# A two-block sequence model on one core: Hyena's convolution by a folded transform at odd frequencies, and the second layer's modulation in the third feed-forward layer

## The chip, the core and the metric

The kernel runs on one core of one Trainium2 chip. A core has a matrix engine (PE, with its weight loads written PEld), a vector engine (DVE), a scalar engine (ACT), a general engine (POOL), and a queue engine (SP) that issues most transfers. The metric is the device time of one execution in microseconds. Three runs of the kernel before took 2188.26, 2190.82 and 2191.55 us; their median is 2190.82.

## The reference

The first block is two layers of feed-forward, a convolution and recurrence mixer, and feed-forward again, on 256 tokens of width 1024. The second block has two layers that are modulated by a condition: an even one (attention and Hyena) and an odd one (mLSTM). The change touches the modulation and Hyena's convolution:

```python
def adaln(cond, w_mod, b_mod):
    m = jax.nn.silu(cond) @ w_mod + b_mod
    return _split(m, (D_MODEL, D_MODEL, D_MODEL))

def bidir_long_conv(u, filt):            # n = 256, filt has 2n taps
    uf = jnp.fft.rfft(u.astype(jnp.float32), n=2 * n, axis=1)
    ff = jnp.fft.rfft(filt, axis=0)
    return jnp.fft.irfft(uf * ff[None], n=2 * n, axis=1)[:, :n].astype(u.dtype)

g = v * x1                               # in hyena_mixer
out = x0 * (bidir_long_conv(g, filt) + g * hy_bias)
```

It is done for 256 latent and 256 context tokens, 1024 channels each, with one filter per channel. The modulation is a product of one vector (the condition, for latents and for the context) with a 1024 x 3072 matrix in each of the two layers.

## The kernel before

Every number is fp32, and a product of two matrices is done as three matrix instructions on halves (`mm3`, lines 127, 128, 129): high by high, high by low, low by high. `split` makes the halves: ACT casts to the high one (L96), DVE subtracts it (L97). `wload` brings 1 MB of weights by one transfer (tile `raw`, two buffers) and splits it into `wh` and `wl` (six buffers each). PSUM banks are in three rings: `mm` (2), `tp` (2, transposes), `acc` (4). A scheduler sets the order of the instructions of each engine from the program and from its own estimates; `weave` and `chain` in the program only say which pieces may lie beside which.

In the trace the stages are: first feed-forward layer 0 to 213 us (beside it the filter's spectrum, `hyena_filter`, four groups of 256 channels, matrix products at 154 to 206); mixer to 464; second feed-forward layer to 655 (beside it the first layer's modulation: 48 reductions in L537, all of them here, although the program gives the second half of them to the third layer); third feed-forward layer to 845; mixer to 1093; fourth feed-forward layer to 1287 (beside it the context's normalization, `ctx_start`); attention to 1495; Hyena to 1835; mLSTM to the end.

`modulation` (line 518) brings the condition (`cb`), forms its silu (ACT L526, DVE L527 and L528) and then takes, for each 128 rows of the transposed matrix (`mraw`, 512 KB each), a multiply-and-sum over 1024 columns in DVE (L537). Its result `mod` scales and shifts the normalized tokens, and gives the gain of the layer's output (`gain_out`, `gain_rows`, through DRAM).

Hyena takes four groups of 256 channels. `project(g)` has eight pieces of 24 matrix instructions (`mm<-HT,w`, 512 columns), each followed by a short convolution on ACT and DVE (`dwconv`) or a gate, and ends in `gg`, the convolution's input, with channels on partitions and 2 x 256 tokens on the free axis. Beside the projection of group g runs the convolution of group g-1: `turn` transposes `gg` (8 transposes, L1001) into `gT`; `forward` multiplies it by cosine and sine tables (`dft`), two halves of frequencies (`kt`) of 12 matrix instructions of 512 columns each, multiplies by the filter's spectrum `F` in DVE (L1019, L1020, L1021) and splits the result into `Y`; `back` multiplies with `Y` as the stationary and the table as the moving operand, 48 matrix instructions of 256 columns, so that channels come back to partitions; ACT scales (`z`, L1040), DVE adds the bias term and the gate (L1041, L1042) and splits `hyo`; `rows` multiplies `hyo` by the output's weights. The second layer's modulation (40 reductions) is woven into groups 0 to 3 too.

The last group has no projection beside it. It goes in two halves of 256 columns, latents and then context; each ends in `next_layer` (line 659), a chain of squares, a power on POOL, a scaling and transposes (L181) that write `HT`, the mLSTM's input. mLSTM's gate products (`acc<-w,HT`) are there to fill PE.

The lines of the profile are those of this kernel:

## Time and profile before

| | us |
|---|---|
| median of three runs | 2190.82 |
| profiled execution, its own time | 2189.3 |
| its span, first to last instruction | 2187.5 |
| PE busy | 2123.8 (97%) |
| PEld busy | 1866.8 (85%) |
| DVE busy | 1595.0 (73%) |
| ACT busy | 1076.1 (49%) |
| POOL busy | 148.0 (7%) |

A matrix instruction's duration in the trace runs over into the next one, which starts before it has ended. What one costs PE is therefore the distance between two starts, which is shorter than the mean duration of a group of rows. [...]

### The profile page before, as it was taken

Reading aid. Unit: us, or ns where it says so; the run is one execution under the profiler, and the core shown is the slowest. Engines: PE = TensorE matmul, PEld = TensorE weight load, DVE = VectorE, ACT = ScalarE, POOL = GpSimd, SP = SyncE. Lnnn points to the kernel's source line nnn. Section 1 sums busy time; section 2 is a strip of 40 time slices with the busy share of each in tenths; the row PEclk is TensorE's granted clock in tenths of the full one; section 3 lists DMA queues with packets and bytes.
Section 4 is the critical chain, followed back from the end, with each engine's and each line's share of the span. In section 5 each row is a group of like instructions: output and inputs, shape, how many; then the busy total and the mean of one; then the engine's idle time right before and its main releaser. Section 6 shows DMA issues by size and latency. Waiting matters only on the chain.

```text
span 2187.5 us, 32454 instructions
## 1 busy us (share of the span) xinstructions
PE 2123.8 (97%) x12945; PEld 1866.8 (85%) x12945; DVE 1595.0 (73%) x2600; ACT 1076.1 (49%) x1650; POOL 148.0 (7%) x137
## 2 busy tenths in 40 slices
PE   8999999999999999999999999999999989999997
PEld 8988897889989997998889976888888867788886
DVE  7665777689977656777576668765898687876766
ACT  5554556544435544575455444544333345565653
POOL 0000221000000000220010012000000022000001
PEclk9999999999999999999999999999999999999999
DMA  8554554567765555546555543114444224233441
GB/s 290 197 185 148 207 188 154 198 240 258 274 248 193 193 186 184 199 154 212 203 187 180 193 161 116 58 40 154 169 159 173 87 75 159 96 116 114 147 141 70
DMA packets 65503, 366.67 MB, mean 168 GB/s; under 512 B 7935, under 2 KB 13128, under 8 KB 27848
## 3 DMA queue, kind: packets, MB, share of 16 engines
q1 hardware_dynamic: 65352, 364.61, 47.5%
q8 instruction: 101, 1.65, 0.3%
q14 instruction: 50, 0.41, 0.1%
HBM read 361.40 MB, written 3.18 MB: 167 GB/s over the span
## 4 chain that ended last, share of the span: by engine, by line
PE 79%; DVE 10%; ACT 4%; POOL 3%; issue 2%; DMA 2%; SPq 0%; POOLq 0%; DVEq 0%; ACTq 0%
PE mm L127 13%; PE mm L128 13%; PE mm L129 13%; PE acc L129 12%; PE acc L128 12%; PE acc L127 12%; DVE wl L97 4%; ACT wh L96 2%; DMA raw<-in_w 1%; PE tp L181 1%; POOL HT L97 1%; DVE v L255 1%; DVE bst L256 1%; PE tp L127 1%; POOL rsv L119 0%
## 5 line engine op out<-in xcount | busy, mean ns | idle before, releaser
L97 DVE TENSOR_TENSOR wl<-raw,wh 128x1024 fp32r<-128x1024 f32 (+1 forms) x566 | 706.3, 1259 | 269.1 <-ACT wh L96 266.4
L96 ACT CAST wh<-raw 128x1024 fp32r<-128x1024 f32 (+1 forms) x590 | 605.7, 1046 | 463.4 <-PE acc L129 153.6
L127 PE MATMUL mm<-xT,wh 128*128 128x256 f32 x1048 | 294.3, 281 | 5.9 <-ACT wh L96 5.9
L129 PE MATMUL mm<-xT,wl 128*128 128x256 f32 x1048 | 294.1, 281 | 3.0 <-POOL wl L97 2.7
L128 PE MATMUL mm<-xT,wh 128*128 128x256 f32 x1048 | 293.6, 280 | 0.0
L129 PE MATMUL acc<-xT,wl 128*128 128x256 f32 x856 | 239.8, 280 | 2.3 <-DVE u L423 1.1
L127 PE MATMUL acc<-xT,wh 128*128 128x256 f32 x856 | 239.9, 280 | 0.7 <-ACT wh L96 0.7
L128 PE MATMUL acc<-xT,wh 128*128 128x256 f32 x856 | 239.5, 280 | 0.0
L127 PEld LDWEIGHTS mm<-xT,wh 128*128 128x128 f32 x1048 | 197.8, 189 | 6.9 <-ACT wh L96 6.3
L129 PEld LDWEIGHTS mm<-xT,wl 128*128 128x128 f32 x1048 | 197.7, 189 | 3.8 <-POOL wl L97 3.1
L128 PEld LDWEIGHTS mm<-xT,wh 128*128 128x128 f32 x1048 | 197.7, 189 | 0.2
L127 PE MATMUL mm<-HT,wh 128*128 128x512 f32 (+1 forms) x448 | 171.2, 382 | 0.9 <-DVE vv L97 0.9
L129 PE MATMUL mm<-HT,wl 128*128 128x512 f32 (+1 forms) x448 | 170.3, 380 | 0.0
L128 PE MATMUL mm<-HT,wh 128*128 128x512 f32 (+1 forms) x448 | 170.2, 380 | 0.0
L129 PEld LDWEIGHTS acc<-xT,wl 128*128 128x128 f32 x856 | 160.9, 188 | 3.1 <-DVE u L423 1.5
L127 PEld LDWEIGHTS acc<-xT,wh 128*128 128x128 f32 x856 | 160.9, 188 | 0.9 <-ACT wh L96 0.9
L128 PEld LDWEIGHTS acc<-xT,wh 128*128 128x128 f32 x856 | 160.9, 188 | 0.0
L127 PE MATMUL acc<-wh,ht 128*128 128x512 f32 x352 | 139.5, 396 | 0.0
L129 PE MATMUL acc<-wh,ht 128*128 128x512 f32 x352 | 139.5, 396 | 0.0
L128 PE MATMUL acc<-wl,ht 128*128 128x512 f32 x352 | 139.3, 396 | 0.0
L127 PE MATMUL mm<-wh,HT 128*128 128x512 f32 x288 | 114.7, 398 | 0.0
L128 PE MATMUL mm<-wl,HT 128*128 128x512 f32 x288 | 114.0, 396 | 0.0
(488 smaller groups left out, 4401.5 us busy)
## 6 DMA issues: line engine op xcount, KB each, us to landing
raw<-in_w SPq DMA_DIRECT2D x131, 1024.0 KB, 4.8
raw<-in_wi_cvb SPq DMA_DIRECT2D x24, 1024.0 KB, 4.8
mraw<-in_w_mod SPq DMA_DIRECT2D x48, 512.0 KB, 4.4
raw<-in_wi_g SPq DMA_DIRECT2D x16, 1024.0 KB, 4.8
raw<-in_e_hy SPq DMA_DIRECT2D x16, 1024.0 KB, 5.1
raw<-in_o_oz SPq DMA_DIRECT2D x16, 1024.0 KB, 4.8
raw<-in_e_out SPq DMA_DIRECT2D x10, 1024.0 KB, 4.8
raw<-in_wi_r SPq DMA_DIRECT2D x8, 1024.0 KB, 4.8
```

Of the source, the lines that this page charges most:

```text
L96: S.copy(h, src)
L97: eng.tensor_tensor(l, src, h.bitcast(F32), op=ALU.subtract)
L127: TE.matmul(p, lhsT=lh, rhs=rh, start=first, stop=False)
L128: TE.matmul(p, lhsT=lh, rhs=rl, start=False, stop=False)
L129: TE.matmul(p, lhsT=ll, rhs=rh, start=False, stop=last)
L181: TE.transpose(tp[:, i * P : (i + 1) * P], b, ident)
L255: V.scalar_tensor_tensor(v[:, c], acc[h], coef, xa[t][:, c], op0=ALU.mult, op1=ALU.add)
L256: V.bn_stats(st[:, h, :], v[:, c])
```

## The change

The transform has odd frequencies, at which the wrap-around of a cyclic convolution comes with the opposite sign, and time is taken apart into even and odd samples. One table of 128 x 128 for each of cosine and sine and for each of even and odd samples then serves both halves of the frequencies: the one half is the sum and the other the difference of the even and the odd part. So

- `forward` has 12 matrix instructions of 512 columns instead of 24 (four `acc` banks); then two copies on ACT, four sums or differences of 512 columns on DVE, the products with `F` (four of 1024 columns, four sums of 512), and two sums or differences of 1024 columns that fold the spectrum, before the four splits of `Y`;
- `back` has the table as the stationary operand: 12 matrix instructions of 512 columns instead of 48 of 256, two copies on ACT into `zt`, and 8 transposes (L1077) that bring channels back to partitions; ACT's `z` reads these and writes every second column;
- `turn` reads every second column of `gg` as its stationary operand, and the filter reads every second column of `hd`;
- the filter's spectrum takes 12 matrix instructions of 256 columns in a group instead of 24, two scalings on ACT, two sums or differences of 512 columns on DVE, and one transfer instead of two;
- the second layer's modulation is the third feed-forward layer's side work, and all of the first layer's is the second's; the second layer's `gain_out` goes from the mLSTM's second head to the fourth feed-forward layer;
- a few tiles (`gb`, `hyo`, `xc`) have other places.

```diff
+    def turned(pool):
+        gain_out(pool.tile([P, P], F32, tag="gr", name="gr"), 1, 0)
+        yield
...
     def dft_tables(pool, n, raw):
 
-        d = [pool.tile([P, 2, n, 256], F32R, tag=f"dft{i}", name=f"dft{i}") for i in range(2)]
-        for k in range(2):
-            for i in range(n // 2):
-                r = raw([P, 2, 256])
-                nc.sync.dma_start(r, a["dft"][:, k, 2 * i : 2 * i + 2])
-                split(d[0][:, k, 2 * i : 2 * i + 2], d[1][:, k, 2 * i : 2 * i + 2], r)
+        d = [pool.tile([P, n, P], F32R, tag=f"dft{i}", name=f"dft{i}") for i in range(2)]
+        for i in range(0, n, 4):
+            m = min(4, n - i)
+            r = raw([P, 2, 256]).rearrange("p a n -> p (a n)")[:, : m * P].rearrange("p (a n) -> p a n", a=m)
+            nc.sync.dma_start(r, a["dft"][:, i : i + m])
+            split(d[0][:, i : i + m], d[1][:, i : i + m], r)
         return d
...
-                        p[:, s * 256 : (s + 1) * 256], hd[:, 0, tsl(pt)], hd[:, 1, tsl(pt)], w3s[:, 0, s, :], w3s[:, 1, s, :],
+                        p[:, s * 256 : (s + 1) * 256], hd[:, 0, pt::2], hd[:, 1, pt::2], w3s[:, 0, s, :], w3s[:, 1, s, :],
...
-            for kt in range(2):
+
+            eo = []
+            for pt in (1, 0):
                 p = psum("tp").rearrange("p (s n) -> p s n", s=2)
                 for s in range(2):
-                    btile(
-                        p[:, s, :],
-                        [(dft[0][:, pt, s, tsl(kt)], dft[1][:, pt, s, tsl(kt)]) for pt in range(2)],
-                        lambda pt: (pq[pt][:, 0, s, :], pq[pt][:, 1, s, :]),
-                    )
-                F = t2([P, 2, 256], "F")
-                S.copy(F, p)
-                nc.sync.dma_start(fdram[g][:, kt], F)
+                    c = 2 * pt + s
+                    mm3(p[:, s, :], dft[0][:, c], dft[1][:, c], pq[pt][:, 0, s, :], pq[pt][:, 1, s, :], True, True)
+                x = t2([P, 2, 256], f"eo{pt}")
+                S.mul(x, p, 1.0 / 256)
+                eo.append(x)
+            F = t2([P, 2, 2, 256], "F")
+            for hf, op in enumerate((ALU.add, ALU.subtract)):
+                V.tensor_tensor(F[:, hf], eo[1], eo[0], op=op)
+            nc.sync.dma_start(fdram[g], F)
...
+        def pair(s, nm):
+            return s.pool.tile([P, 2, 512], F32, tag="pr", name=nm, bufs=4)
+
         def turn(s, g, segs, gT):
 
             for t in range(2):
                 tp = psum("tp")
                 for i, st in enumerate(segs):
                     for j in range(2):
-                        TE.transpose(tp[:, i * 256 + j * P :][:, :P], s.gg[g][j][:, st * T + t * P :][:, :P], ident)
+                        TE.transpose(
+                            tp[:, i * 256 + j * P :][:, :P], s.gg[g][j][:, st * T + t : (st + 1) * T : 2], ident
+                        )
                 split(gT[t][:, 0, :], gT[t][:, 1, :], tp[:, : 256 * len(segs)])
 
         def forward(s, n, gT, Y, bank="acc"):
 
-            seg = lambda x: x.rearrange("p (s n) -> p s n", s=n)
-            for kt in range(2):
-                u = []
+
+            w = 256 * n
+            ps = {}
+            for t in (1, 0):
                 for x in range(2):
-                    p = psum(bank)[:, : 256 * n]
-                    btile(
-                        p, [(s.dft[0][:, t, x, tsl(kt)], s.dft[1][:, t, x, tsl(kt)]) for t in range(2)],
-                        lambda t: (gT[t][:, 0, :], gT[t][:, 1, :]),
-                    )
-                    u.append(seg(p))
-                Fb = [s.F[:, kt, x, :].unsqueeze(1).broadcast_to([P, n, 256]) for x in range(2)]
-                for x, op in ((0, ALU.subtract), (1, ALU.add)):
-                    pr = [s.pool.tile([P, 512], F32, tag="pr", name="pr", bufs=3)[:, : 256 * n] for i in range(2)]
-                    V.tensor_tensor(seg(pr[0]), u[0], Fb[x], op=ALU.mult)
-                    V.tensor_tensor(seg(pr[1]), u[1], Fb[1 - x], op=ALU.mult)
-                    V.tensor_tensor(pr[0], pr[0], pr[1], op=op)
-                    split(Y[kt, x][:, 0, :], Y[kt, x][:, 1, :], pr[0])
-                yield
+                    ps[t, x] = p = psum(bank)[:, :w]
+                    c = 2 * t + x
+                    mm3(p, s.dft[0][:, c], s.dft[1][:, c], gT[t][:, 0, :], gT[t][:, 1, :], True, True)
+            u = [s.pair("u") for _ in range(2)]
+            for x in range(2):
+                S.copy(u[1][:, x, :w], ps[1, x])
+            for x in range(2):
+                V.tensor_tensor(u[0][:, x, :w], ps[0, x], u[1][:, x, :w], op=ALU.add)
+                V.tensor_tensor(u[1][:, x, :w], ps[0, x], u[1][:, x, :w], op=ALU.subtract)
+            yield
+            m = [s.pair("m") for _ in range(2)]
+            seg = lambda x: x[:, :, :w].rearrange("p x (s n) -> p x s n", s=n)
+            for hf in range(2):
+                for i in range(2):
+                    F = s.F[:, hf, ::-1] if i else s.F[:, hf]
+                    V.tensor_tensor(seg(m[i]), seg(u[hf]), F.unsqueeze(2).broadcast_to([P, 2, n, 256]), op=ALU.mult)
+                for x, op in enumerate((ALU.subtract, ALU.add)):
+                    V.tensor_tensor(u[hf][:, x, :w], m[x][:, 0, :w], m[x][:, 1, :w], op=op)
+            yield
+            for t, op in enumerate((ALU.add, ALU.subtract)):
+                V.tensor_tensor(m[t][:, :, :w], u[0][:, :, :w], u[1][:, :, :w], op=op)
+                for x in range(2):
+                    Y[t, x] = y = s.spec(w)
+                    split(y[:, 0, :], y[:, 1, :], m[t][:, x, :w])
+            yield
+
...
         def back(s, g, segs, Y, hy):
 
             n = len(segs)
+            w = 256 * n
             c = slice(256 * segs[0], 256 * (segs[-1] + 1))
+            zt = s.pair("zt")
+            for t in range(2):
+                p = psum("acc")[:, :w]
+                for x in range(2):
+                    k = 2 + x if t else 4 + x
+                    mm3(p, s.dft[0][:, k], s.dft[1][:, k], Y[t, x][:, 0, :], Y[t, x][:, 1, :], x == 0, x == 1)
+                S.copy(zt[:, t, :w], p)
+            yield
+            zz = s.pair("z")
             for j in range(2):
-                p = psum("acc")[:, : 256 * n]
+                tp = psum("tp")
                 for i in range(n):
-                    b = slice(i * 256 + j * P, i * 256 + (j + 1) * P)
-                    btile(
-                        p[:, i * T : (i + 1) * T],
-                        [(Y[kt, x][:, 0, b], Y[kt, x][:, 1, b]) for kt in range(2) for x in range(2)],
-                        lambda k: (s.dft[0][:, k // 2, 2 + k % 2, :], s.dft[1][:, k // 2, 2 + k % 2, :]),
-                    )
-                z = s.pool.tile([P, 512], F32, tag="pr", name="z", bufs=3)[:, : 256 * n]
+                    for t in range(2):
+                        TE.transpose(tp[:, (2 * i + t) * P :][:, :P], zt[:, t, i * 256 + j * P :][:, :P], ident)
+                z = zz[:, j, :w]
                 f = 2 * g + j
-                S.activation(z, p, AF.Identity, scale=il1[:, g, 2 * j : 2 * j + 1])
+                S.activation(
+                    z.rearrange("p (s n a) -> p s a n", s=n, a=2), tp[:, :w].rearrange("p (s a n) -> p s a n", s=n, a=2),
+                    AF.Identity, scale=il1[:, g, 2 * j : 2 * j + 1],
+                )
                 V.scalar_tensor_tensor(z, s.gg[g][j][:, c], fvc[:, 12, f : f + 1], z, op0=ALU.mult, op1=ALU.add)
                 V.tensor_tensor(z, z, s.x0g[g][j][:, c], op=ALU.mult)
                 split(hy[j][:, 0, c], hy[j][:, 1, c], z)
@@ -1050,7 +1093,7 @@
             gT = [s.gh("gT") for _ in range(2)]
             s.turn(g, (0, 1), gT)
             yield
-            Y = {(kt, x): s.gh("Y") for kt in range(2) for x in range(2)}
+            Y = {}
...
-                pooled("md", lambda p: modulation(p, 0, range(0, 6), 3)),
-                pooled("md", lambda p: modulation(p, 0, range(6, 12), 3)),
+                pooled("md", lambda p: modulation(p, 0, range(12), 3)),
+                pooled("md", lambda p: modulation(p, 1, range(12), 3)),
...
-                    side = ctx_start(ht)
+                    side = chain(ctx_start(ht), pooled("go", turned))
...
-            hy.dft = dft_tables(pool, 4, lambda sh: hy.t2("dr"))
-            mods = modulation(pool, 1, range(12), 1)
-            weave(hy.project(0), mods, 2)
+            hy.dft = dft_tables(pool, 6, lambda sh: hy.t2("dr"))
+            run(hy.project(0))
             for g in range(1, 4):
-                weave(hy.project(g), paired(chain(hy.convolve(g - 1), *([hy.rows(g - 1)] if g < 3 else [])), mods))
-            run(mods)
-
-            gb = pool.tile([P, D], F32, tag="mraw", name="gb", bufs=1)
+                weave(hy.project(g), chain(hy.convolve(g - 1), *([hy.rows(g - 1)] if g < 3 else [])))
...
-            if h == 1:
-                gain_out(pool.tile([P, 256], F32, tag="hn", name="gr", bufs=1), 1, 0)
...
-    k = np.arange(n)
-    ang = 2.0 * np.pi * (np.outer(k, k) % (2 * n - 1)) / (2 * n - 1)
-    wk = np.where(k == 0, 1.0, 2.0)[:, None] / (2 * n - 1)
-    dft = np.stack([np.cos(ang), np.sin(ang), wk * np.cos(ang), wk * np.sin(ang)]).astype(f32)
-    o["dft"] = dft.reshape(4, 2, P, n).transpose(2, 1, 0, 3)
+    k = np.arange(P)
+    tab = []
+    for odd in range(2):
+        ang = np.pi * (np.outer(2 * k + odd, 2 * k + 1) % (4 * n)) / (2 * n)
+        tab += [np.cos(ang), np.sin(ang)]
+    tab += [x.T for x in tab[:2]]
+    o["dft"] = np.stack(tab).astype(f32).transpose(1, 0, 2)
```

Three places of the instruction order. First DVE at Hyena's first convolution, between the forward and the back products. Before (`cv`: the short convolution; `mod`: the reduction's result; `pr`, `Y`: the first half of the frequencies):

```order
L1020 TENSOR_TENSOR pr<-acc,F 128x512
L537 ISA cjunk,mod<-mraw,cb 128x1024
L537 ISA mod 128x1
L1021 TENSOR_TENSOR pr<-pr 128x512
L1019 TENSOR_TENSOR pr<-acc,F 128x512
L1020 TENSOR_TENSOR pr<-acc,F 128x512
L97 TENSOR_TENSOR Y<-pr,Y 128x512
L1021 TENSOR_TENSOR pr<-pr 128x512
```

Now (`u`: even and odd part and then the halves of the spectrum; `m`: products and then the folded spectrum):

```order
L1040 TENSOR_TENSOR u<-m 128x512
L691 SCALAR_TENSOR_TENSOR cv_15604<-mm,fvc,cv_15604 128x2x255
L1040 TENSOR_TENSOR u<-m 128x512
L692 SCALAR_TENSOR_TENSOR cv_15604<-mm,fvc,cv_15604 128x2x255
L1038 TENSOR_TENSOR m<-u,F 128x1024 x2
L994 TENSOR_TENSOR gg<-cv_15604,cv_15541 128x512
L1040 TENSOR_TENSOR u<-m 128x512 x2
L989 SCALAR_TENSOR_TENSOR x0g<-x0g,mm 128x512
L1043 TENSOR_TENSOR m<-u 128x1024
L990 SCALAR_TENSOR_TENSOR x0g<-x0g,cv_15494 128x512
L1043 TENSOR_TENSOR m<-u 128x1024
L97 TENSOR_TENSOR Y<-m,Y 128x512 x4
```

The reductions have gone from here, the first half's split no longer comes before the second half's products, and all four splits of `Y` stand at the end. On PE, 72 projection matrix instructions stand between the last of the forward and the first of the back products; before, 24 stood between the two halves of the forward and 24 between the second half and the back.

Second, DVE at the start of the third feed-forward layer, just behind the normalization that ends the second. Before (`xT`: the transposed input's low half; `h`: the first gates):

```order
L269 SCALAR_TENSOR_TENSOR v<-v,rs,lnb 128x512 x2
L97 TENSOR_TENSOR wl<-raw,wh 128x1024
L97 TENSOR_TENSOR xT<-tp,xT 128x4x128
L97 TENSOR_TENSOR wl<-raw,wh 128x1024
L97 TENSOR_TENSOR xT<-tp,xT 128x4x128
L97 TENSOR_TENSOR wl<-raw,wh 128x1024
L295 SCALAR_TENSOR_TENSOR h<-h,mm 128x256
```

Now:

```order
L269 SCALAR_TENSOR_TENSOR v<-v,rs,lnb 128x512 x2
L97 TENSOR_TENSOR wl<-raw,wh 128x1024
L97 TENSOR_TENSOR xT<-tp,xT 128x4x128
L527 TENSOR_SCALAR mraw<-mraw 128x1024
L97 TENSOR_TENSOR xT<-tp,xT 128x4x128
L528 TENSOR_TENSOR cb<-cb,mraw 128x1024
L527 TENSOR_SCALAR mraw<-mraw 128x1024
L537 ISA cjunk,mod<-mraw,cb 128x1024
L537 ISA mod 128x1
L295 SCALAR_TENSOR_TENSOR h<-h,mm 128x256
```

The silu of the condition and the first reduction have come between the two splits of `xT` and ahead of the first gates.

Third, PE at the end of Hyena, where the latents' transposes for mLSTM (`tp<-ident,j`) meet the context half's back products (`acc` with `Y`). Before:

```order
L181 MATMUL tp<-ident,j 128x128 x8
L129 MATMUL mm<-wh,hyo 128x512
L128 MATMUL acc<-dft_15116,Y 128x256
L129 MATMUL acc<-dft_15115,Y 128x256
L127 MATMUL acc<-dft_15115,Y 128x256
L128 MATMUL acc<-dft_15116,Y 128x256
L129 MATMUL acc<-dft_15115,Y 128x256
L127 MATMUL acc<-dft_15115,Y 128x256
L128 MATMUL acc<-dft_15116,Y 128x256
L129 MATMUL acc<-dft_15115,Y 128x256
L127 MATMUL acc<-wh,HT 128x512
L181 MATMUL tp<-ident,j 128x128 x8
```

Now:

```order
L181 MATMUL tp<-ident,j 128x128 x16
L127 MATMUL acc<-Y,dft_15173 128x256 x2
L127 MATMUL acc<-wh,HT 128x512
L128 MATMUL acc<-wl,HT 128x512
L129 MATMUL acc<-wh,HT 128x512
L128 MATMUL acc<-Y,dft_15173 128x256
L129 MATMUL acc<-Y,dft_15174 128x256
L127 MATMUL acc<-Y,dft_15173 128x256
L128 MATMUL acc<-Y,dft_15173 128x256
L129 MATMUL acc<-Y,dft_15174 128x256
```

The latents' two blocks of eight transposes, which stood ten instructions apart with back products between them, stand in one block of sixteen, and all twelve back products of the half behind it.

## Rows read from the trace of the kernel before

**Rows 1.** The page: busy us (share of the span) and instructions of each engine.
```profile
PE 2123.8 (97%) x12945; PEld 1866.8 (85%) x12945; DVE 1595.0 (73%) x2600; ACT 1076.1 (49%) x1650; POOL 148.0 (7%) x137
```

**Rows 2.** Waits, 1495 to 1755: engine line, waited for, us, times, longest.
```profile
PE mm L127 <- DVE x0g L982: 0.4, 1, 0.4
```

**Rows 3.** Windows, one Hyena period: us, busy us (instructions) by engine, granted clock.
```profile
1563.96:1632.20 68.24, 68.24 (x323) 56.04 (x321) 64.92 (x99) 21.75 (x28) 0.00 (x0) 1.00 0.42 151
```

**Rows 4.** Windows, L537 alone in the same period.
```profile
1563.96:1632.20 68.24, 23.48 (x39) 1.00 0.42 151
```

**Rows 5.** Timeline of PE, first convolution: start us, us, engine, line, operation.
```profile
1563.80 1.04 PE L1001 MATMUL tp<-ident,gg 128*128 128x128 f32 x8
1564.60 0.47 PE L127 MATMUL mm<-HT,wh 128*128 128x512 f32 x1
...
1570.29 0.39 PE L127 MATMUL acc<-gT,dft 128*128 128x512 f32 x1
1570.52 0.40 PE L128 MATMUL acc<-gT,dft 128*128 128x512 f32 x1
...
1587.11 0.28 PE L128 MATMUL acc<-dft,Y 128*128 128x256 f32 x1
1587.23 0.28 PE L129 MATMUL acc<-dft,Y 128*128 128x256 f32 x1
```

**Rows 6.** Instructions on the tile gT: duration ns min/median/max, starts, forms.
```profile
L127 PE MATMUL acc<-gT,dft x40: 276/389/395, 1570.3 to 1770.1; 128*128 128x512 f32 x24, 128*128 128x256 f32 x16
```

**Rows 7.** Windows, the filter groups beside the first feed-forward layer.
```profile
154.00:206.00 52.00, 52.00 (x296) 43.66 (x295) 31.36 (x54) 24.77 (x36) 0.00 (x0) 1.00 0.52 175
```

**Rows 8.** Timeline of DVE, two pairs that follow each other.
```profile
1568.58 1.23 DVE L97 TENSOR_TENSOR wl<-raw,wh 128x1024 fp32r<-128x1024 f32 x1
1569.72 1.22 DVE L537 CUSTOM_DVE_ANT_0 cjunk<-mraw,cb 128x1024 bf16<-128x1024 f32 x1
...
1759.29 0.69 DVE L681 TENSOR_TENSOR ys<-ys,mm 128x512 f32<-128x512 f32 x1 [0.45 <-PE mm L129]
1759.90 0.42 DVE L97 TENSOR_TENSOR Y<-pr,Y 128x256 fp32r<-128x256 f32 x1
```

**Rows 9.** Instructions on the tile Y, in ACT.
```profile
L96 ACT CAST Y<-pr x20: 392/612/623, 1578.1 to 1795.1; 128x512 fp32r<-128x512 f32 x12, 128x256 fp32r<-128x256 f32 x8
```

**Rows 10.** Timeline of DVE, starts of the residual sum at three layer ends.
```profile
462.50 1.23 DVE L528 TENSOR_TENSOR cb<-cb,mraw 128x1024 f32<-128x1024 f32 x1
463.64 1.28 DVE L255 SCALAR_TENSOR_TENSOR v<-acc,xa 128x512 f32<-128x512 f32 x2
...
654.66 1.38 DVE L255 SCALAR_TENSOR_TENSOR v<-acc,xa 128x512 f32<-128x512 f32 x2 [2.56 <-PE acc L129]
...
845.10 1.40 DVE L255 SCALAR_TENSOR_TENSOR v<-acc,xa 128x512 f32<-128x512 f32 x2 [5.35 <-PE acc L129]
```

**Rows 11.** Windows of 30 us in the second and the third feed-forward layer.
```profile
510.00:540.00 30.00, 30.00 (x257) 30.00 (x257) 28.13 (x45) 14.49 (x22) 0.00 (x0) 1.00 0.68 239
700.00:730.00 30.00, 30.00 (x257) 30.00 (x257) 18.56 (x26) 15.00 (x21) 0.00 (x0) 1.00 0.55 195
```

**Rows 12.** Instructions on the tile mraw, in DVE.
```profile
L537 DVE CUSTOM_DVE_ANT_0 cjunk<-mraw,cb x88: 1207/1219/1228, 466.0 to 1684.8; 128x1024 bf16<-128x1024 f32 x88
...
L527 DVE TENSOR_SCALAR mraw<-mraw x6: 684/690/696, 459.9 to 1524.5; 128x1024 f32<-128x1024 f32 x6
```

**Rows 13.** Waits, 1755 to 1840.
```profile
PE acc L127 <- ACT Y L96: 5.1, 2, 4.8
```

**Rows 14.** Windows, the end of the Hyena stage.
```profile
1784.00:1790.00 6.00, 1.16 (x9) 0.95 (x7) 5.56 (x10) 4.94 (x12) 4.10 (x4) 0.74 0.00 0
1760.00:1835.00 75.00, 60.50 (x291) 48.61 (x290) 57.28 (x109) 40.00 (x86) 25.93 (x24) 0.93 0.30 105
```

**Rows 15.** Timeline of PE at the lower clock.
```profile
1800.93 0.63 PE L127 MATMUL acc<-wh,HT 128*128 128x512 f32 x1
1801.36 0.63 PE L128 MATMUL acc<-wl,HT 128*128 128x512 f32 x1
```

More of the change, by code (lines that the diff above doesn't have):

```diff
@@ L870, in hyena_filter @@
         b4 = lambda sh, nm, n: pool.tile(sh, F32R, tag=nm, name=nm, bufs=n)
-        dft = dft_tables(pool, 2, lambda sh: t2(sh, "dr"))
+        dft = dft_tables(pool, 4, lambda sh: t2(sh, "dr"))
         zt, fw1, fw2, fvec = t2([33, 256], "zt"), t2([33, 64], "fw1"), t2([64, 64], "fw2"), t2([64, 3], "fvec")
@@ L950, in __init__ @@
             s.pool, s.ht, s.ys = pool, ht, ys
-            s.x0g, s.gg, s.hy = {}, {}, {}
+            s.x0g, s.gg, s.hy, s.half = {}, {}, {}, None
         def t2(s, nm):
@@ new lines, in forward, with spec @@
+            yield
[5 more added lines that the diff above has]
+            yield
+        def spec(s, w):
+            if w == 512:
+                return s.gh("Y")
+            if s.half is None:
+                s.half = s.gh("Y")
+                return s.half[:, :, :w]
+            y, s.half = s.half[:, :, w:], None
+            return y
@@ L1403, in body @@
             flat = lambda x: x.rearrange("p s n -> p (s n)")
[L1404 to L1406 removed]
+            hy.dft = dft_tables(pool, 6, lambda sh: hy.t2("dr"))
+            run(hy.project(0))
             for g in range(1, 4):
[L1408 to L1411 removed]
+                weave(hy.project(g), chain(hy.convolve(g - 1), *([hy.rows(g - 1)] if g < 3 else [])))
+            gb = pool.tile([P, D], F32, tag="gb", name="gb", bufs=1)
             gain_rows(gb, 0, 0)
@@ L1415, in body @@
             gT = [[x[:, :, t * 256 : (t + 1) * 256] for t in range(2)] for x in gT]
-            hyo = pool.tile([P, 2, 2, 512], F32R, tag="cb", name="hyo")
+            hyo = pool.tile([P, 2, 2, 512], F32R, tag="hyo", name="hyo")
             hyo = [hyo[:, j] for j in range(2)]
-            def spectrum():
-                Y = [hy.gh("Y") for _ in range(2)]
-                return {(kt, x): Y[kt][:, :, x * 256 : (x + 1) * 256] for kt in range(2) for x in range(2)}
             halves = lambda: [flat(hy.t2("j")) for _ in range(2)]
@@ L1425, in body @@
                 hy.turn(3, (st,), gT[st])
-            Y = spectrum()
+            Y = {}
             run(hy.forward(1, gT[0], Y), hy.back(3, (0,), Y, hyo), hy.rows(2, "mm", range(2)), hy.rows(3, "mm", range(2)))
@@ L1430, in body @@
             run(hy.rows(2, "mm", range(2, 4)))
-            Y = spectrum()
+            Y = {}
             run(hy.forward(1, gT[1], Y), hy.back(3, (1,), Y, hyo))
@@ L1435, in body @@
             run(hy.rows(3, "mm", range(2, 4)))
-            xc = pool.tile([P, 2, D], F32, tag="dft0", name="xc")
-            load_ctx([xc[:, t, :] for t in range(NT)])
+            xc = [hy.pair("xc").rearrange("p a n -> p (a n)") for _ in range(NT)]
+            load_ctx(xc)
             for t in range(NT):
-                next_layer(ys[2 + t], gb, xc[:, t, :], t, 1, 1, ht, halves())
+                next_layer(ys[2 + t], gb, xc[t], t, 1, 1, ht, halves())
         ozp = right.enter_context(new_pool("oz", side="right"))
@@ L1571, in _layout @@
     deltas = np.linspace(math.log(1e-2) / 1.5, math.log(1e-2) / 0.3, D, dtype=f32)
-    o["decay"] = np.exp(-t * np.abs(deltas)).astype(f32).reshape(2, P, D).transpose(1, 0, 2)
+    o["decay"] = np.exp(-t * np.abs(deltas)).astype(f32).reshape(P, 2, D)
     inv = np.power(f32(10000.0), -np.arange(32, dtype=f32) / f32(32)).astype(f32)
```

## The prediction

> **What bounds the kernel now.** I read the page's first part, the waits of PE by stretch, windows over single stages, and then the timelines of PE and DVE. PE is busy for 97% of the span, with every other engine below it [rows 1]. In the Hyena stage up to 1755 us PE waits for 0.4 us in all [rows 2], and one period of a Hyena group, from one group's transposes to the next's, is 68.24 us with PE busy in all of it at the full clock [rows 3]. A busy PE says little by itself, since durations run into each other, so I count by the distance of starts: 0.23 us for 512 columns, 0.12 us for 256, and 0.80 us from the first of eight transposes to the instruction behind them [rows 5]. By these distances the period's work is 192 projection instructions (44.2), 8 transposes (0.8), 24 forward instructions (5.5), 48 back instructions (5.8) and 48 output instructions (11.0), together 67.3 of the 68.24 us. PE is fed there, and an instruction that goes from it is time that goes. The same holds beside the first feed-forward layer, where the filter's products lie: PE is busy for 52.00 of 52 us [rows 7]. It does not hold at the end of Hyena: from 1760 to 1835 PE is busy for 60.5 of 75 us at a mean clock of 0.93 [rows 14].
>
> **The change part by part.** The sum is made against the profiled execution's own 2189.3 us (span 2187.5, and 1.8 around it). The median of the runs shown is 1.5 us above it, and I add that at the end.
>
> Filter: four groups lose 12 instructions of 256 columns each; 48 x 0.12 = 5.8 us. What is added (two sums of 512 columns on DVE in a group, 1.2 us at the 0.61 us between starts of [rows 8]) is covered, since DVE is busy for 31 of the 52 us [rows 7]. If the chain showed at the end of the groups, the price would be these 1.2 us for the last one. Minus 5.8.
>
> Forward in the three full groups: the 24 instructions of 512 columns (their x24 for three groups in one of the three lines are in [rows 6], so 72 in all) become 12. 3 x 12 x 0.23 = 8.3 us. Minus 8.3.
>
> Back in the three full groups: 48 x 0.12 = 5.8 becomes 12 x 0.23 = 2.8 and eight transposes. For those I have 0.80 by starts and 1.04 by their own span [rows 5] and take 0.9. 3 x (5.8 - 2.8 - 0.9) = 6.3 us. Minus 6.3.
>
> The chain in between is the price. On PE 72 projection instructions stand between the last forward and the first back product: 72 x 0.23 = 16.6 us of cover. DVE has to do in this time four sums of 512 columns, six instructions of 1024, four sums of 512, and six of the projection's own of 512. By the distance of starts (1.14 for 1024, 0.61 for 512 columns [rows 8]) that is 2.4 + 6.8 + 2.4 + 3.7 = 15.3 us; ACT's cast of 0.61 [rows 9] may begin one 1.14 earlier, so the first high half is there after 14.8 us and its low half after 15.9 us, just in time. By the full durations in the same rows (1.23 and 0.69) DVE takes 17.0 us, the low half is there after 17.7 us, and PE stands for 1.1 us. That is, between 0 and 1.1 for each of three; starts are the better measure, the margin is thin, and I take 0.4. Plus 1.2. Over a whole period DVE has room: it is busy for 64.92 of 68.24 us [rows 3], loses 23.48 us of reductions [rows 4] and gains 4.4 (the sums and products above are 11.7 where twelve instructions of 512 columns took 7.3), which makes some 46 of then 63.7 us (68.2 - 2.8 - 2.1 + 0.4). The steps' DMAs are the same, with one F load in a group as before.
>
> [...]
>
> The last group in two halves: PE loses 12 instructions of 256 columns in each forward and 12 in each back and gains four transposes (half of 0.9), 2 x (24 x 0.12 - 0.45) = 4.9 us. But PE is idle there for 14.5 us [rows 14], most of it in two waits, one of 4.8 us for a cast of Y [rows 13], and the order puts the latents' sixteen transposes into one block ahead of the context half's back products. So the gain is 4.9 if the chain gets as much shorter, and a loss of 5 if the sixteen transposes hold the back products for as long as the cast does now. I take minus 1, nearest to a wait that only moves.
>
> Modulation in the third feed-forward layer: 40 reductions of 1.22 us [rows 12], 49 us of DVE. The layer's DVE is busy for 18.6 of 30 us, and in the second layer, which has 48 reductions, for 28.1 of 30, with the same 257 instructions on PE [rows 11]. From residual sum to residual sum the second layer takes 191.0 us and the third 190.4 [rows 10]: 48 hidden reductions cost 0.6. At the layer's start one silu instruction of 0.69 us [rows 12] now stands between the two splits of xT, with the next layer's first products waiting for the second split. I take 0.6 + 0.7, plus 1.3. Its bounds are 0, and 5.1 if both silus (0.69 and 1.23 each [rows 10, 12]) and one reduction come onto the path, as one of the silu's instructions stands right before the residual sum at 463.64 [rows 10]. The cond and mraw transfers go into SP's queue between weight transfers; that happens in the second layer already.
>
> gain_out in the fourth feed-forward layer instead of in mLSTM, the places of tiles, the smaller tables: one transpose, one scaling, and one transfer that nobody waits for until the end. The cover is a fed PE. 0, with 2 either way.
>
> Sum: -5.8 - 8.3 - 6.3 + 1.2 - 1.0 + 1.3 = -18.9, so 2170.4 for the profiled execution and **2172** on the scale of the median. With the bounds of the terms (chain 0 to 3.3, end -5 to +5, modulation 0 to 5.1, small things 2 either way, not all at one end) the forecast's own range is 2166 to 2178.
>
> **The rivals.**
> The chain is late (chance 0.13). DVE's order is fixed, and the next piece's weight subtractions stand behind the four splits of Y. If the chain goes by full durations and two weight subtractions of 1.14 us are late behind it, each convolution stands for 1.1 + 2.3 = 3.4 us, 9 us more than in my sum, and with the end at +5 instead of -1 the time is 2187. For it: the margin of 0.7 us above. Against it: before, DVE was fuller, and PE waited for 0.4 us in the stage.
>
> Strided weight loads (0.08). The transposes of gg and the filter's products on hd read every second column as their stationary operand; no row of before has such a load. If it doubled the distance to the next start, 32 transposes cost 0.10 more each (0.80 for eight) and 48 filter products 0.12 more, 9 us: 2181. If it cost nothing, the sum stands, and I take that, since weight loads lie beside the products (PEld 1866.8 us beside PE's 2123.8 [rows 1]) and the period's products alone fill it. [...]
>
> The modulation is not hidden (0.05). The third layer's gates come late at its start and its weights after that, as the DVE near its limit in the second layer would let one expect: 5 to 10 us, 2176 to 2181.
>
> More gain (0.08). The end's chain shortens by the full 4.9 us or more, no convolution stands: below 2166.
>
> Slower (0.06). PE idles for longer at the end of Hyena, before the block of sixteen transposes, and its clock falls. [...] Today that is short: the mean clock over those 75 us is 0.93 [rows 14]. [...] Against it: the block has 48 output instructions ahead of it, 11 us of cover.
>
> **How the numbers follow.** Forecast 0.60, more gain 0.08, late chain 0.13, strided loads 0.08, modulation 0.05, slower 0.06. What a measurement here can tell from no change is 0.2%, 4.4 us: faster is below 2186.4, slower above 2195.2. Faster: 0.60 + 0.08 + 0.08 + 0.05 and half of the late chain, 0.87. The other half of it is no change, 0.07. Slower 0.06. The range is 2164 to 2187: it leaves out about half of the case of more gain, part of the late chain above its price, and the slow case.
>
> **What would show it.** The period from one group's transposes (now L1011) to the next's should be near 63.7 us with PE busy in all of it; a late chain shows as PE waits for Y's cast or subtraction there, before the first back product. The filter's stretch should have PE busy throughout and the first feed-forward layer end near 207 instead of 213. Eight strided transposes should still move the next start by 0.80. The third layer should last for 191 to 192 us between residual sums, with no PE wait for gates at its start. The forecast is wrong if PE waits for more than 3 us between the Hyena transposes, or if the stretch from the last group's transposes to the first mLSTM head grows.

## The result, and the profile after

The changed kernel took 2169.59 us (median of six runs, 2158.91 to 2176.51; the kernel before on the same chip 2190.47). The ratio is 0.9899, 95% interval 0.9871 to 0.9927. The profiled execution took 2166.9 us, span 2165.1, so 22.4 less than before.

The page's first part, as in [rows 1]:

```profile
PE 2096.4 (97%) x12737; PEld 1840.8 (85%) x12737; DVE 1604.5 (74%) x2611; ACT 1077.3 (50%) x1665; POOL 149.3 (7%) x137
```

PE is busy for 27 us less and is 97% of the span as before. By stage, each from one residual sum (L255) or one group's first transposes (L1001, now L1011) to the next, us in the two profiled executions, one of each kernel:

| stage | before | after | difference | forecast |
|---|---|---|---|---|
| first feed-forward, with the filter | 213.1 | 207.3 | -5.8 | -5.8 |
| first mixer | 250.5 | 248.1 | -2.4 | 0 |
| second feed-forward | 191.0 | 192.0 | +1.0 | with the third |
| third feed-forward | 190.4 | 190.2 | -0.3 | +1.3 |
| second mixer | 248.0 | 247.9 | -0.1 | 0 |
| fourth feed-forward | 193.6 | 191.5 | -2.1 | 0 |
| attention to the first transposes | 277.1 | 277.1 | 0 | 0 |
| two Hyena periods and the last projection | 188.0 | 173.5 | -14.5 | -13.4 |
| last group in halves, and mLSTM | 435.6 | 437.5 | +1.9 | -1.0 |

Windows over the two periods, columns as in [rows 3]:

```profile
1554.06:1617.49 63.43, 63.43 (x281) 51.31 (x280) 48.17 (x62) 23.50 (x32) 0.00 (x0) 1.00 0.24 85
1617.49:1680.94 63.45, 63.45 (x281) 51.36 (x280) 48.17 (x62) 23.52 (x32) 0.00 (x0) 1.00 0.26 92
```

The period is 63.4 us instead of 68.2 and PE is busy in all of it; from 1486 to 1727 no PE row stands among the waits at all. DVE is at 48.2 of 63.4. The timeline of DVE and then of PE at the first convolution (start us, us):

```profile
1563.53 0.68 DVE L1030 TENSOR_TENSOR u<-acc,u 128x512 f32<-128x512 f32 x1
1564.13 0.74 DVE L692 SCALAR_TENSOR_TENSOR cv<-mm,fvc,cv 128x510 f32<-128x510 f32 x1
1564.79 0.68 DVE L1031 TENSOR_TENSOR u<-acc,u 128x512 f32<-128x512 f32 x1
...
1570.05 0.75 DVE L691 SCALAR_TENSOR_TENSOR cv<-mm,fvc,cv 128x510 f32<-128x510 f32 x1 [0.26 <-ACT cv L690]
...
1578.49 1.22 DVE L1043 TENSOR_TENSOR m<-u 128x1024 f32<-128x1024 f32 x1
1579.62 2.49 DVE L97 TENSOR_TENSOR Y<-m,Y 128x512 fp32r<-128x512 f32 x4
...
1580.22 0.39 PE L127 MATMUL acc<-Y,dft 128*128 128x512 f32 x1
...
1580.92 0.39 PE L128 MATMUL acc<-Y,dft 128*128 128x512 f32 x1
```

From the first sum to the first split of Y are 16.1 us from start to start; PE does not wait before the first back product. A window over the filter, as in [rows 7], and one of the three lines of the transform's products in the whole layer, before and after:

```profile
150.00:202.00 52.00, 52.00 (x264) 41.78 (x263) 38.37 (x64) 25.31 (x36) 0.00 (x0) 1.00 0.50 175
...
L127 PE MATMUL tp<-pq,dft x32: 277/281/384, 154.4 to 202.1; 128*128 128x256 f32 x32
L127 PE MATMUL tp<-pq,dft x16: 279/298/365, 156.1 to 204.9; 128*128 128x256 f32 x16
```

PE is busy in all of the window, as before. The transform's products are 48 in the layer instead of 96; from start to next start, the 96 took 12.0 us in all and the 48 take 6.8, so 5.2 less.

The end of Hyena is where the forecast failed. PE's waits there, before and after, and the window from the last group's first transposes to the first product of mLSTM's first head (`mm<-HT`), before and after:

```profile
PE tp L181 <- DVE j L583: 4.4, 3, 3.0
PE tp L181 <- DVE j L587: 11.7, 3, 7.7
...
PE acc L127 <- ACT Y L96: 6.2, 2, 3.1
...
1751.84:1833.88 82.04, 67.17 (x330) 54.19 (x329) 63.23 (x121) 42.07 (x91) 24.81 (x23) 0.94 0.29 102
1727.57:1812.41 84.84, 63.80 (x290) 50.29 (x289) 71.55 (x131) 47.82 (x107) 28.48 (x24) 0.90 0.28 101
```

The same instructions lie in both windows but for the 40 that the halves lost (48 products less 8 transposes, 4.9 us in the forecast). PE is busy for only 3.4 us less, at a mean granted clock of 0.90 instead of 0.94 (shares of full speed), and idle for 21.0 us instead of 14.9. So the window is 2.8 us longer and not shorter; what lies behind it takes 0.9 less. PE's timeline, the blocks of eight transposes, before and then after:

```profile
1782.59 1.09 PE L181 MATMUL tp<-ident,j 128*128 128x128 f32 x8 [0.24 <-DVE j L583]
1790.61 1.97 PE L181 MATMUL tp<-ident,j 128*128 128x128 f32 x8
1829.67 1.09 PE L181 MATMUL tp<-ident,j 128*128 128x128 f32 x8 [3.00 <-DVE j L583]
```

```profile
1759.99 1.06 PE L181 MATMUL tp<-ident,j 128*128 128x128 f32 x8
1768.73 1.97 PE L181 MATMUL tp<-ident,j 128*128 128x128 f32 x8 [7.67 <-DVE j L587]
1773.77 1.19 PE L127 MATMUL acc<-Y,dft 128*128 128x256 f32 x2 [3.07 <-ACT Y L96]
1774.76 0.63 PE L127 MATMUL acc<-wh,HT 128*128 128x512 f32 x1
1775.19 0.63 PE L128 MATMUL acc<-wl,HT 128*128 128x512 f32 x1
...
1803.77 1.09 PE L181 MATMUL tp<-ident,j 128*128 128x128 f32 x8 [2.84 <-DVE j L587]
```

Counted from the first transposes, the latents' two blocks come at 32.4 and 41.2 us instead of 30.8 and 38.8, the context's last at 76.2 instead of 77.8: the chain to the latents' second block has grown by 2.4 us, and the whole up to the last eight has shrunk by 1.6. The two waits on either side of the second block are 7.7 and 3.1 us, and after them 512 columns are 0.43 us apart, as in [rows 15], at a granted clock of 0.50 (1774.76 to 1778.00). Of the gate's products (`acc<-w,HT`), 63 lie ahead of the last eight transposes instead of 82, and the rest follows behind them.

### The profile page after: what moved, and what is told of

Same layout as the page of the kernel before. It is cut to its first block, busy times and chain, and to the rows that moved or that the text cites. A ratio compares the mean times of both kernels' runs of the same rounds, so it can differ in the third digit from the quotient of the medians.

```text
span 2165.1 us, 32034 instructions
## 1 busy us (share of the span) xinstructions
PE 2096.4 (97%) x12737; PEld 1840.8 (85%) x12737; DVE 1604.5 (74%) x2611; ACT 1077.3 (50%) x1665; POOL 149.3 (7%) x137
```

## The experiments

All kernels but one are the changed kernel with an edit. "First transposes" are those of the last group (L1011), from which the end is counted.

**after_again and after_control**: no edit, two more sets of five and six runs.

> The changed kernel once more, unaltered, for its scatter and for a second trace. Theory (the gain is PE work that went): the ratio to the kernel before is again 0.988 to 0.992, the Hyena periods are again 63.4 us, and the first feed-forward layer ends again near 207.3. Open are two stages that came out shorter without being touched: the first mixer by 2.4 us and the fourth feed-forward layer by 2.1. If tile places or the instruction order make them shorter, they are 248.1 and 191.5 again; if they differ from run to run, at least one of them is 1 us or more longer here.

> The changed kernel unaltered on the same chip, as the measure for the two others: a ratio to the kernel before of 0.989 to 0.992, Hyena periods of 63.4 us, and the latents' first eight transposes 32.4 us after the last group's first.

Medians 2169.71 and 2169.49, ratios 0.9911 (0.9894 to 0.9928) and 0.9908 (0.989 to 0.9927). Hyena periods are 63.42 and 63.43, first transposes to the latents' eight 32.4 and 32.7, first transposes to the end 441.6 and 437.8. The first mixer is 248.1 and 247.9, the fourth feed-forward layer 191.8 and 195.0, the third 187.3 and 187.8, the first 208.0 and 210.8. So feed-forward layers differ by 3 us and more between executions of one kernel, the end of the kernel by 4, and Hyena's periods by 0.02. The windows of the third layer in after and, second, in after_again (the first bracket holds PE's instructions):

```profile
723.00:753.00 30.00, 30.00 (x257) 30.00 (x256) 30.00 (x51) 13.62 (x22) 0.00 (x0) 1.00 0.77 273
```

```profile
723.00:753.00 30.00, 30.00 (x267) 30.00 (x267) 30.00 (x50) 15.21 (x23) 0.00 (x0) 1.00 0.81 290
```

Same work, a granted clock of 1.00, PE busy throughout, and 257 or 267 instructions of 256 columns in 30 us. That is part of the scatter; whether it is all of it is not shown. Either way a feed-forward layer's 2 us cannot be put down to the change. The first mixer was 247.7 to 248.4 in every other trace, move_only's with the old convolution included; what stands out is the one execution of [rows 10] with its 250.5.

Of the end's 4 us, 2.8 stand in one stretch, in which TensorE's granted clock differed. From the last eight transposes to the first head, in after and in after_again:

```profile
1803.77:1812.41 8.64, 8.64 (x42) 7.13 (x43) 8.49 (x16) 6.51 (x15) 4.08 (x2) 1.00 0.58 195
```

```profile
1801.15:1812.59 11.44, 11.44 (x41) 9.43 (x42) 9.44 (x17) 6.91 (x15) 3.18 (x2) 0.73 0.63 231
...
1801.15 1.97 PE L181 MATMUL tp<-ident,j 128*128 128x128 f32 x8 [2.84 <-DVE j L587]
```

PE had waited 2.84 us just before in both. In the one the granted clock stayed at 1.00, in the other it was 0.73 on the mean, and the same instructions took 11.44 us instead of 8.64, 2.8 more.

**pe_twice**: gives PE the instructions of the filter and the forward back.

```diff
-                    mm3(p[:, s, :], dft[0][:, c], dft[1][:, c], pq[pt][:, 0, s, :], pq[pt][:, 1, s, :], True, True)
+                    for _ in range(2):
+                        mm3(p[:, s, :], dft[0][:, c], dft[1][:, c], pq[pt][:, 0, s, :], pq[pt][:, 1, s, :], True, True)
...
-                    mm3(p, s.dft[0][:, c], s.dft[1][:, c], gT[t][:, 0, :], gT[t][:, 1, :], True, True)
+                    for _ in range(n):
+                        mm3(p, s.dft[0][:, c], s.dft[1][:, c], gT[t][:, 0, :], gT[t][:, 1, :], True, True)
```

> The changed kernel with each forward product of the three full groups and each of the filter's transform products done twice (the second overwrites the first with the same numbers), which gives PE back the instructions that the fold took there. Theory (PE sets the time in both places): Hyena periods 63.4 + 12 x 0.23 = 66.2 us, and the first feed-forward layer 48 x 0.12 = 5.8 us longer than the 207 to 209.5 of the changed kernel and its variants. Rival (the fold's DVE chain has become the bound of a period): periods below 65.

Periods are 66.15 us (+2.7, for 12 instructions of 0.23), the first layer 215.0, the time of the single run 2184.04. In a period PE's instructions are the price, and the chain through DVE is not the bound. The first layer goes the same way, but it scatters (207.3 to 210.8 in the three traces of the changed kernel), so that its 48 instructions are shown there only to some 2 us.

**move_only** (the kernel before with the modulation and gain moved) and **mod_back** (the changed kernel with them where they were). The edit shown is mod_back's:

```diff
-                pooled("md", lambda p: modulation(p, 0, range(12), 3)),
-                pooled("md", lambda p: modulation(p, 1, range(12), 3)),
+                pooled("md", lambda p: modulation(p, 0, range(0, 6), 3)),
+                pooled("md", lambda p: modulation(p, 0, range(6, 12), 3)),
...
+            mods = modulation(pool, 1, range(12), 1)
+            weave(hy.project(0), mods, 2)
...
+                weave(hy.project(g), paired(chain(hy.convolve(g - 1), *([hy.rows(g - 1)] if g < 3 else [])), mods))
+            run(mods)
...
```

> The old convolution and filter, with the second layer's modulation in the third feed-forward layer and its gain in the fourth. Theory (the modulation was hidden before too, PE sets the time): within 3 us of the kernel before, Hyena periods 68.1, the third feed-forward layer longer by 0 to 1. Rival (DVE's relief, or the condition's silu that no longer stands before a residual sum, carries part of the gain): 4 us or more faster than before.

> The new convolution and filter, but the second layer's modulation put back into Hyena and the gain back into mLSTM, as in the kernel before. Theory (DVE room): the first Hyena period's DVE work is then about 45.9 + 23.5 = 69 us against a PE period of 63.4, so PE waits there for 5 us or more and a little in the second period; the whole is 5 to 10 us slower than the changed kernel, near 2176 us. Rival (the reductions fit beside the folded transform as well, and the move of the modulation is worth nothing): within 2 us of the changed kernel, with periods of 63.4.

move_only: ratio 0.9986 (0.9972 to 1.0001), periods 68.4, the second and third feed-forward layers 191.4 and 190.4 (191.0 and 190.4 before), the latents' first block at 30.7 us. The move alone is worth nothing that shows. mod_back: 2179.12, ratio 0.9950 (0.9932 to 0.9968), above the changed kernel's intervals. mod_back's windows over the first 125 us of the same stretch:

```profile
1561.56:1624.00 62.44, 59.97 (x264) 47.65 (x263) 60.81 (x92) 21.48 (x30) 0.00 (x0) 1.00 0.36 125
1624.00:1687.00 63.00, 59.15 (x257) 46.55 (x256) 61.38 (x90) 23.37 (x32) 0.00 (x0) 1.00 0.54 192
```

DVE is busy for all but 1.6 us of each and PE waits 2.5 and 3.9; the stretch that takes 173.5 us is 182.4 here. The reductions were free beside a PE period of 68 us and are not beside one of 63: the move has no price of its own, but without it 9 of the fold's 14.5 us in Hyena are lost. Its end has the changed kernel's 32.4, 41.1 and 76.2 us, so what happens there belongs to the fold and not to the move.

**no_stride**: contiguous operands, for the transposes of `gg` and for the filter's products on `hd`. What is convolved is then another order of samples.

```diff
-                            tp[:, i * 256 + j * P :][:, :P], s.gg[g][j][:, st * T + t : (st + 1) * T : 2], ident
+                            tp[:, i * 256 + j * P :][:, :P], s.gg[g][j][:, st * T + t * P :][:, :P], ident
...
-                        p[:, s * 256 : (s + 1) * 256], hd[:, 0, pt::2], hd[:, 1, pt::2], w3s[:, 0, s, :], w3s[:, 1, s, :],
+                        p[:, s * 256 : (s + 1) * 256], hd[:, 0, tsl(pt)], hd[:, 1, tsl(pt)], w3s[:, 0, s, :], w3s[:, 1, s, :],
```

> The changed kernel with contiguous instead of every second column read for the stationary operands of the transposes of gg and of the filter's products on hd (what is convolved is then another order of samples). Theory (strided loads are longer but hidden): the weight loads of these transposes go from 208 ns back to 140, and the Hyena periods stay within 0.2 us of 63.4. Rival (each strided load costs its length): periods shorter by 0.5 us or more.

Weight loads of these transposes and one block of eight with the instruction behind it, in after and in no_stride (ns min/median/max; then start us, us):

```profile
L1011 PEld LDWEIGHTS tp<-ident,gg x32: 195/208/209, 1553.8 to 1732.0; 128*128 128x128 f32 x32
...
1554.06 1.11 PE L1011 MATMUL tp<-ident,gg 128*128 128x128 f32 x8
1554.93 0.47 PE L127 MATMUL mm<-HT,wh 128*128 128x512 f32 x1
```

```profile
L1011 PEld LDWEIGHTS tp<-ident,gg x32: 138/140/143, 1558.6 to 1736.5; 128*128 128x128 f32 x32
...
1558.84 1.04 PE L1011 MATMUL tp<-ident,gg 128*128 128x128 f32 x8
1559.63 0.48 PE L127 MATMUL mm<-HT,wh 128*128 128x512 f32 x1
```

The strided load takes 208 ns instead of 140, and eight cost 0.87 us instead of 0.79; the period goes from 63.43 to 63.35. The strided loads are longer here, but nearly all of that lies beside other work.

**ctx_mid**: the context half's products between the latents' two tiles.

```diff
-            for t in range(NT):
-                next_layer(ys[t], gb, xa[t], t, 1, 0, ht, halves())
-            run(hy.rows(2, "mm", range(2, 4)))
+            next_layer(ys[0], gb, xa[0], 0, 1, 0, ht, halves())
             Y = {}
             run(hy.forward(1, gT[1], Y), hy.back(3, (1,), Y, hyo))
+            next_layer(ys[1], gb, xa[1], 1, 1, 0, ht, halves())
+            run(hy.rows(2, "mm", range(2, 4)))
```

> The changed kernel with one move at the end of Hyena: the context half's forward and back products come in the program between the two latent tiles' next_layer and not behind both, so that PE's order has eight transposes, the twelve back products, and then the other eight transposes. Theory (PE's fixed order makes the back products wait 7.7 us for the second block of transposes): the end is 5 to 8 us shorter and less of it is at the lower clock, near 2162 us. Rival (DVE, which is busy nearly throughout there, sets the end): within 2 us of the changed kernel.

2169.20, ratio 0.9902 (0.9882 to 0.9922): no difference that can be told from the changed kernel, where the theory wanted 5 to 8 us. The last eight transposes come 74.4 us after the first transposes instead of 76.2, and from there to the end it takes 362.6 where the changed kernel took 361.3 to 365.0. PE's fixed order is not what costs.

**tail_less_dve**: less vector work in the halves (in `forward`, where `n` is 1): two differences and the two folds are left out, so that the result is another one.

```diff
-                V.tensor_tensor(u[1][:, x, :w], ps[0, x], u[1][:, x, :w], op=ALU.subtract)
+                if n == 2:
+                    V.tensor_tensor(u[1][:, x, :w], ps[0, x], u[1][:, x, :w], op=ALU.subtract)
...
-                V.tensor_tensor(m[t][:, :, :w], u[0][:, :, :w], u[1][:, :, :w], op=op)
+                if n == 2:
+                    V.tensor_tensor(m[t][:, :, :w], u[0][:, :, :w], u[1][:, :, :w], op=op)
...
```

> The changed kernel without part of the fold's vector work in the last group's two halves alone: two differences of 256 columns and two folds of 512 are left out in each half (the output is another one), 1.9 us of DVE in each by distances of starts. Theory (the end of Hyena is a chain through DVE, to which the fold adds): from the last group's first transposes the latents' first eight transposes come after 30.5 us instead of 32.4 and the second after 38 to 39 instead of 41.2. Rival (POOL's powers and splits or the transfers set that chain): both within 0.5 us of 32.4 and 41.2.

PE's timeline, first transposes and the latents' two blocks:

```profile
1729.23 0.63 PE L1011 MATMUL tp<-ident,gg 128*128 128x128 f32 x4
...
1758.13 1.06 PE L181 MATMUL tp<-ident,j 128*128 128x128 f32 x8
...
1766.86 1.54 PE L181 MATMUL tp<-ident,j 128*128 128x128 f32 x6 [7.54 <-DVE j L587]
```

28.9 and 37.6 us instead of 32.4 and 41.2: both 3.5 earlier, more than the 1.9 that were expected. In DVE's order the context half's two differences lie ahead of these blocks too, which makes 2.6; the last 0.9 is not traced. The first head comes after 78.4 us instead of 84.8, with PE idle for 17.2 instead of 21.0, and first transposes to the end is 431.6 us (437.5 to 441.6 in the changed kernel). That the chain through DVE sets the latents' blocks, and that the fold's sums lengthen it, is shown.

**ht_on_dve**: DVE in place of POOL.

```diff
-        split(d[:, :, 0, :], d[:, :, 1, :], xn.rearrange("p (k n) -> p k n", k=4), G)
+        split(d[:, :, 0, :], d[:, :, 1, :], xn.rearrange("p (k n) -> p k n", k=4))
```

> The changed kernel with the subtraction of the HT halves on DVE instead of POOL (it touches the start of attention too). Theory (POOL's splits, 3 to 7.5 us for two, hold up the next tile's power on POOL at the end of Hyena): the last eight transposes come 2 to 3 us earlier than the 76.2 after the last group's first, and the time is 2 to 4 us below the changed kernel. Rival (DVE, which gets 0.6 us for each of eight more, is what the end waits for): the same or slower.

Last transposes after 75.9 instead of 76.2: the theory fell, POOL's splits do not hold the end up. At attention's start 1.7 us are saved (275.4 instead of 277.1). Ratio 0.9893 (0.9875 to 0.9911), which overlaps the changed kernel's intervals.

**tail_unfold** and **tail_unfold_ht**: in the halves PE does the sums. `forward_sums` stands in for `forward` where `n` is 1, `back` takes all four Y for each of even and odd, and two negated tables are added.

```diff
+        def forward_sums(s, gT, Y, bank):
+            for hf in range(2):
+                p = psum(bank).rearrange("p (x n) -> p x n", x=2)
+                for x in range(2):
+                    o = 6 + x if hf else 2 + x
+                    mm3(p[:, x, :], s.dft[0][:, x], s.dft[1][:, x], gT[0][:, 0, :], gT[0][:, 1, :], True, False)
+                    mm3(p[:, x, :], s.dft[0][:, o], s.dft[1][:, o], gT[1][:, 0, :], gT[1][:, 1, :], False, True)
...
+                        k = (6 + x if hf else 2 + x) if t else 4 + x
+                        mm3(p, s.dft[0][:, k], s.dft[1][:, k], Y[hf, x][:, 0, :], Y[hf, x][:, 1, :], i == 0, i == 3)
```

> The changed kernel with the fold taken back in the last group's two halves only, where PE is idle: the sums and differences of even and odd parts are accumulated by PE (with two more tables, the odd ones negated), 24 more instructions of 256 columns in each half, and four sums and two folds of DVE (2.5 us by distances of starts) and two copies of ACT fall away in each; the output is the same. Theory (the end is a chain through DVE that the fold lengthens, and PE has room): the latents' first eight transposes come 3 to 4 us earlier after the last group's first than the 32.4, the last eight 2 to 4 us earlier than 76.2, and the time is 2 to 6 us below the changed kernel's. Rival (PE's added 5.6 us count, as they do in a period): the same or slower than the changed kernel.

> As tail_unfold, and with the subtraction of the HT halves on DVE instead of POOL. Theory: the 1.7 us that this gave at the start of attention come on top, so 1 to 2 us below tail_unfold; at the end of Hyena it changes nothing by itself. Rival (with the chain through DVE shorter, the eight subtractions that DVE gets now lengthen it): not faster than tail_unfold.

PE's timeline of tail_unfold, first transposes, the latents' first and the context's last block:

```profile
1717.63 0.63 PE L1011 MATMUL tp<-ident,gg 128*128 128x128 f32 x4
...
1746.81 0.95 PE L181 MATMUL tp<-ident,j 128*128 128x128 f32 x7
...
1787.16 1.09 PE L181 MATMUL tp<-ident,j 128*128 128x128 f32 x8 [3.07 <-DVE j L587]
```

29.2 us instead of 32.4, and 69.5 (69.1 in tail_unfold_ht) instead of 76.2: with 5.6 us more for PE the chain is 3.2 and 6.7 us shorter. First transposes to the end is 436.4 and 433.1 us, against 437.5 to 441.6: most of what the chain gains goes again on PE's added work and on what then lies behind the last transposes. The times are 2164.63 and 2165.32, ratios 0.9890 (0.9870 to 0.9909) and 0.9887 (0.9868 to 0.9906), against 0.9908 (0.9890 to 0.9927) of the unaltered kernel on the same chip. Both are faster than the kernel before. That they are faster than the changed one is not shown: the intervals overlap, and the two profiled executions, the fastest of their six, owe much of it to feed-forward layers (203.5, 187.7 and 186.7 us for tail_unfold's first three). Nor is tail_unfold_ht 1 to 2 us below tail_unfold, as its theory had it, although the 1.7 us at attention's start are there again (275.3).

## Why the prediction was right, and where a term was not

The time, the sign and, but for the end, the mechanism held: 18.9 us forecast, 22.4 between the two profiled executions and 20.9 between the medians. That the sum comes so close is in part luck, since a feed-forward layer alone scatters by 3 us.

Filter: 5.8 forecast, 5.8 found in the stage. The agreement to a tenth is chance, as the stage took 207.3 to 210.8 in the changed kernel; the 48 products less make 5.2 by their own distances, and pe_twice's layer goes back up with them.

Forward and back in the full groups: 8.3 + 6.3 = 14.6 forecast, 14.5 found. The term for the chain, plus 1.2, was too much: PE waits at no convolution. The trace has 16.1 us up to the first split of Y, where distances of starts had given 15.3 and full durations 17.0; 0.26 of the 16.1 is a wait for ACT that neither counted. Full durations would have had PE wait, which no row shows. The rows go by starts: the one at 1564.79 us starts 0.08 before the one ahead of it ends (1564.13 and 0.74).

The end: the step that failed is "so the gain is 4.9 if the chain gets as much shorter ... I take minus 1, nearest to a wait that only moves". The wait did not only move, it grew: PE lost 40 instructions there and was idle for 6.2 us more up to the first head. I had counted the halves' PE products and not the vector work that the fold adds to each half (four sums and two folds, 2.5 us by starts), in a stretch where PE waits for DVE. tail_less_dve and tail_unfold show that this work delays the latents' blocks; how much of the 6.2 us is its share, and how much PE's lost filling, is not taken apart. By the prediction's own sign the stretch from the last group's transposes to the first mLSTM head should not grow; it grew by 2.8 us. The term came out at plus 1.9 in the profiled execution and plus 2.1 and 6.0 in the two repeats, the last of them outside the bounds of 5 either way. The slower rival's mechanism is there in small: the second block waits 7.7 us and the granted clock behind it is 0.50 over 14 instructions (1774.76 to 1778.00), and in after_again it is lower once more behind the last block, 0.73 on the mean over 41. It would have taken some 95 instructions, at 0.20 us more each (512 columns 0.43 us apart instead of 0.23), to cost the 18.9 us of the forecast.

Modulation: plus 1.3 forecast, plus 0.7 over the second and third layers found, and three executions of the same third layer lie 2.8 us apart: not to be told from nothing. For the same reason the 0.6 us that the prediction read as the price of 48 hidden reductions, from two layers of one execution, is no price. What I had not seen is that the place of the reductions decides over Hyena's gain (mod_back).

Strided loads: the rival's mechanism is there at 0.08 us for eight transposes instead of 0.8, a tenth of its price; for the filter's products the scatter of their layer (207.3 to 210.8 us) hides it. The load's own time is 208 ns against 140, though the instruction behind the eight starts only 0.08 us later (0.87 us against 0.79).

Beyond the sum: 4.5 us of the 22.4 stand in the first mixer, which the change does not touch, and in the fourth feed-forward layer, where it only puts `gain_out`. The mixer's part comes from the one execution before; the fourth layer took 191.5 to 195.0 us in the three traces of the changed kernel, so its part is within the scatter. Without them the profiled difference is 17.9. How far a median of six evens them out is not shown.

## What to carry over

Where PE is busy throughout, count its instructions at the distance of starts; in Hyena they came out to a tenth of a microsecond. Where PE waits, count what the change adds to the engine that it waits for, even if that engine has less to do over the whole stage. And when one engine's period gets shorter, look again at the work that another one had hidden beside it.

## What the runs showed of the hardware

In 30 us of the third feed-forward layer (723 to 753 us), at a granted clock of 1.00 and with PE busy throughout, PE did 257 instructions of 256 columns in one execution of the changed kernel and 267 in another. What chooses the pace stays open. The weight load of a 128 x 128 fp32 operand that takes every second column of `gg` took 208 ns instead of 140 (medians of 32, after and no_stride). After the same wait of 2.84 us the granted clock up to the first head was 1.00 in after and 0.73 on the mean in after_again, and the stretch took 8.64 and 11.44 us. In after, instructions of 512 columns started 0.43 us apart at a granted clock of 0.50 (1774.76 and 1775.19 us) and 0.23 apart at 1.00 (1805.17 and 1805.40 us).
